# Paired heads in the first mixer, joint chunk operands in the second, and no spin matmuls

## The chip, the cores and the metric

The kernel runs on one core of one Trainium2 chip. The metric is the device time of one execution in microseconds (us), as the median over runs. Engines are written PE (TensorE; PEld is its weight load), DVE (VectorE), ACT (ScalarE), POOL (GpSimd) and SP (SyncE). L553 is line 553 of the kernel's source.

## The reference, cut to what matters

The model is a two-layer backbone over 256 context tokens and 256 latent tokens of width 1024. Layer 0 mixes tokens with a bidirectional Mamba-2 scan and then applies a SwiGLU; layer 1 mixes with bidirectional RWKV-7 and then applies 8 experts of which each token uses 2. For one chunk of 128 tokens and one head the first mixer computes

```python
seg = cum[:, :, :, None] - cum[:, :, None, :]
decay = jnp.exp(jnp.where(lower, seg, -jnp.inf))
cb = jnp.einsum('bcign,bcjgn->bcijg', cm, bm)
w = cb[..., None] * decay * dt[:, :, None]
y = jnp.einsum('bcijge,bcjgep->bcigep', w, x)
```

in each direction, over 32 heads of 64 channels. The second mixer is a recurrence over tokens with a 64x64 state per head (16 heads, two directions, first over the context and then, from the state it left, over the latents):

```python
sa = jnp.einsum('bhvk,bhk->bhv', S, kk_t)
S = S * w_t[:, :, None, :] - sa[..., None] * b_t[:, :, None, :] + v_t[..., None] * k_t[:, :, None, :]
```

## The kernel before, in words

All matmuls are fp32 or a three-product split of fp32 into two fp32r parts. An fp32 matmul stands in the trace as two PE instructions, one for each pass; a PE transpose is one. A tile framework makes the order on each engine: it takes the program's instructions by priority (earlier in the program first) as they become ready in a timeline that it simulates, and it places every semaphore. Tiles of one name in one pool share `bufs` buffers, and the next tile of the name waits until the last reader of the buffer is done.

**First mixer** (L467 to L595). Four groups g, two halves s of each. `project` multiplies a weight slab with the 512 tokens (L212 to L214); `wsplit` makes the two fp32r parts of a slab, the high one on ACT (L206), the low one on the engine it is given (L207): `XE` for the x slabs, `ZE` for the gate slabs. `mix` handles two pairs of heads (m) of its half. For each head e of a pair and each direction d it makes the decays `E` (two bf16 matmuls into `pbc`, then four ACT exponentials, L548), multiplies them with `cb` on DVE into `W` (L550), and adds four matmuls, one for each chunk c, into the PSUM bank `py` (L553). Head e uses the 64 columns of the array that write partitions 64e to 64e+63.

**Second mixer** (L717 to L1567). Heads go in two halves hh of four head pairs; "par" says which head of a pair, and its 64 partitions. Chunks have 64 tokens. The stage generator `stage` runs once for each direction d: `lora` makes rates for two chunks, `decays` makes the running sums `cum` and the decays `Dp`, `operands` makes the tile `BK` (per head two 64-column blocks, from `ta` on DVE at L1060 and from `kd` on POOL at L1061, one instruction for each par) and `KR`, and `grams` multiplies them (L1077 for the latents, L1080 for the context), masks the products into `C` (L1084), and transposes `BK` into `BT` (L1089). `dc` holds each chunk's last decay (L1053). `invert` inverts unit-triangular chunk matrices: a DVE part (L1167, L1170), then three rounds of small 32x32 matmuls (L1197, L1211, L1225). `scan` carries the state through the four chunks. `weave` interleaves generators. The order of the stretches: features and stage of context half 0; its `invert` (called with `warm=(2, 4)`) woven with the stage of context half 1; its scan; features of the latents woven with the inversion and scan of half 1; then for the latents stage 0, inversion 0 woven with the value projection, scan 0 woven with stage 1, inversion 1, scan 1.

With `warm` set, `invert` puts a matmul of the identity (`spin`, L1116: 128x128 weights, 128 columns, fp32) ahead of every second n of the first round and every fourth n of the others, into a part of the PSUM bank that the round itself writes afterwards or doesn't use: 32 in all.

Behind the mixers come the experts (from L1690 on), which stream 1 MB weight tiles through SP's DMA queue; their first loads are issued when the second mixer's pools close.

Of the kernel before, what the change touches and what calls it, by code (L numbers as in the profile page):

```python
# [21 lines left out]
NT = 512  # L22
# [115 lines left out]
def tile_backbone(ctx: ExitStack, tc: tile.TileContext, T, out: bass.AP, dbg=None, stop=99):  # L138
# [227 lines left out]
    with ExitStack() as es:  # L366
# [102 lines left out]
        LATE = ((0, 0), (0, 0), (0, 1), (2, 0))  # L469
        XE, ZE = (V,), (G,)  # L470
        ORDER = ((0, 1, 2, 3), (1, 0, 3, 2))
# [24 lines left out]
        def mix(g, s, px, bf, cf, btm, cb):  # L496
# [38 lines left out]
            for m in range(2):  # L535
                mi = 4 * g + 2 * s + m
                py = bank("py", 1)
                for e in range(2):
                    h = hf + 2 * m + e
                    for d in range(2):  # L540
                        pbc = bank("pbc", 2)
                        PE.matmul(pbc, ehb[:, h:h + 1].to_broadcast([96, 128]), parts[d], start=True, stop=False)
                        PE.matmul(pbc, identb, maskb[:, d:d + 1, :].to_broadcast([128, 4, 128]),
                                  start=False, stop=True)
                        E = mt.tile([128, NT], F32, name="E")
                        for c in range(4):
                            sl = slice(128 * c, 128 * c + 128)
                            S.activation(E[:, sl], pbc[:, sl], AF.Exp, bias=ncum[:, c, 32 * d + h:32 * d + h + 1])  # L548
                        W = mt.tile([128, NT], F32, name="W")
                        V.tensor_mul(W, E, cb)  # L550
                        for c in range(4):
                            sl = slice(128 * c, 128 * c + 128)
                            PE.matmul(py[64 * e:64 * e + 64, sl], xdt[d][:, c, 128 * m + 64 * e:128 * m + 64 * e + 64],  # L553
                                      W[:, sl], start=d == 0 and c == 0, stop=d == 1 and c == 3,
                                      skip_group_check=True)
                V.tensor_add(yz[:, mi, :], yz[:, mi, :], py)
                for d in range(2):
                    h = hf + 2 * m
                    pbc = bank("pbc", 2)
                    PE.matmul(pbc, ehw[:, h:h + 2, :].rearrange("p h q -> p (h q)"), parts[d],  # L560
                              start=True, stop=True)
                    E = mt.tile([128, NT], F32, name="E")
                    S.activation(E, pbc, AF.Exp)
                    p = misc()
                    cs = [c for c in range(4) if c != FIRST[d]]
                    for c in cs:
                        sl = slice(128 * c, 128 * c + 128)
                        PE.matmul(p[:, sl], st[d][c][:, 128 * m:128 * m + 128], cf[:, sl], start=True, stop=True)
                    W = mt.tile([128, NT], F32, name="W")
                    for sl in ((slice(128, 512),) if d == 0 else (slice(0, 128), slice(256, 512))):  # L570
                        V.tensor_mul(W[:, sl], E[:, sl], p[:, sl])
                        V.tensor_add(yz[:, mi, sl], yz[:, mi, sl], W[:, sl])

# [418 lines left out]
    def stage(tp, rp, F, un, d, l2, nb, bks, tags, ready):  # L992
# [4 lines left out]
        o = 1 - d  # L997
        last = 64 if d == 0 else 0
        gr, ms = (lambda: bank(tags[0], 2)), (lambda: bank(tags[1], 2))
# [36 lines left out]
        def decays(c):  # L1036
            th = cur[c // 2][0]
            cum = tp.tile([128, 4, 64], F32, name=f"cum{d}", bufs=nb)
            e = 1 if d == 0 else -1
            V.tensor_tensor_scan(cum.rearrange("p k t -> p (k t)")[:, ::e], smask.rearrange("p k t -> p (k t)"),  # L1040
                                 th[:, c % 2].rearrange("p k t -> p (k t)")[:, ::e], 0.0, op0=ALU.mult, op1=ALU.add)
            Dp = tp.tile([128, 4, 65], F32, name=f"Dp{d}", bufs=nb)
            G.memset(Dp[:, :, 64 * d:64 * d + 1], 1.0)
            S.activation(Dp[:, :, o:o + 64], cum, AF.Exp, scale=-0.3032655)
            S.activation(cum, cum, AF.Exp, scale=0.3032655)
            return Dp, cum

        def operands(c, dd, slot):
            Dp, Di = dd
            _, ta, kd = cur[c // 2]  # L1050
            cs = slice(64 * c, 64 * c + 64)
            cl = slice(64 * (c % 2), 64 * (c % 2) + 64)
            V.tensor_copy(un.dc[d][:, :, c:c + 1], Dp[:, :, last:last + 1])  # L1053
            KR = rp.tile([128, 4, NQ], F32, name=f"KR{slot}")

            BK = bks[d][un.flip[d]]
            un.flip[d] ^= 1
            for par in range(2):
                r, b0 = ROWS[par], 64 * par
                V.scalar_tensor_tensor(BK[par][r, :, b0:b0 + 64], ta[r, :, cl], 0.5, Di[r], op0=ALU.mult, op1=ALU.mult)  # L1060
                G.tensor_mul(BK[par][r, :, 64 - b0:128 - b0], kd[r, :, cl], Di[r])  # L1061
            V.tensor_mul(KR[:, :, 0:64], F["kk"][:, ks, cs], Dp[:, :, d:d + 64])
            if j:
                V.tensor_mul(KR[:, :, 64:128], F["r"][:, ks, cs], Dp[:, :, o:o + 64])
            un.KR[d][c] = KR
            return BK

        def grams(c, BK, slot):
# [5 lines left out]
            for h in range(4):  # L1074
                for par in range(2):
                    if j:
                        PE.matmul(g[par][:, h, :], BK[par][:, h, :], KR[:, h, :], start=True, stop=True)  # L1077
                    else:
                        for z in range(2):
                            PE.matmul(g[par][ROWS[z], h, :], BK[par][:, h, 64 * z:64 * z + 64], KR[:, h, :],  # L1080
                                      start=True, stop=True)
            for par in range(2):
# [4 lines left out]
            for h in range(4):  # L1087
                for par in range(2):
                    PE.transpose(t[par][:, 64 * h:64 * h + 64], BK[par][ROWS[par], h, :],  # L1089
                                 ident[ROWS[par], ROWS[par]])  # L1090
            BT = rp.tile([128, 2, 4, 64], F32, name=f"BT{slot}")
# [21 lines left out]

    def spin(o, x):

        PE.matmul(o[:, :x.shape[1] * x.shape[2]], ident, x, start=True, stop=True)  # L1116

    def invert(tp, un, zbank, slots={}, warm=(0, 0)):


# [68 lines left out]
        for d in range(2):  # L1189
            zb = zbank() if d else z0  # L1190
            z = zb[:, :256].rearrange("p (n t) -> p n t", t=16)
            for n in range(16):
                if warm[0] and n % warm[0] == 0:
                    spin(zb[:, 256:], zp[:, d, n, 0:16].unsqueeze(2).to_broadcast([128, 16, 8]))
                for q in range(4):
                    a, b = (TB[1], zp[:, 1, :, 0:16]) if d else (zp[:, 0], T32[0][:, :, 16:32])
                    PE.matmul(z[QS(q), n, :], a[QS(q), n, :], b[QS(q), n, :], start=True, stop=True)  # L1197
# [5 lines left out]
        for d in range(2):  # L1203
            cb_ = slice(32 * (1 - d), 32 * (1 - d) + 32)
            z = zbank()
            for n in range(16):
                if warm[1] and n % warm[1] == 0 and n < 13:
                    spin(z[:, 32 * n:], TB[d][:, n, :].unsqueeze(2).to_broadcast([128, 32, 4]))
                for par in range(2):
# [7 lines left out]
        for d in range(2):  # L1217
            cb_ = slice(32 * (1 - d), 32 * (1 - d) + 32)
            z = zbank()
            for n in range(16):  # L1220
                if warm[1] and n % warm[1] == 0 and n < 13:
                    spin(z[:, 32 * n:], T32[d][:, n, :].unsqueeze(2).to_broadcast([128, 32, 4]))
                for par in range(2):
                    qa, qb = QA(d, par), QA(1 - d, par)
                    PE.matmul(z[qa, 32 * n:32 * n + 32], zs[qb, d, n, :], T32[d][qb, n, :], start=True, stop=True)  # L1225
# [82 lines left out]
    def operand_tiles(tp):  # L1308
        t = [[tp.tile([128, 2, 4, 128], F32, name=f"BK{d}{i}") for i in range(2)] for d in range(2)]
        for d in t:  # L1310
            for x in d:
                for par in range(2):
                    G.memset(x[:, par], 0.0)
        return [[[x[:, par] for par in range(2)] for x in d] for d in t]

# [16 lines left out]
    with ExitStack() as es:  # L1332
# [28 lines left out]
        with tc.tile_pool(name="r00", bufs=1, side="right", reuse_waits="tile") as r00, tc.tile_pool(name="tp0", bufs=1, reuse_waits="tile") as tp:  # L1361
# [21 lines left out]
            mark("A01T00")  # L1383
            weave((invert(tp, D0, misc, warm=(2, 4)), 1), *stages(tp, r01, F, D1, 1, bks, (("gr", "xu"), ("acc", "xu")), always))
            mark("T01S00")
            slots = {"T": ("BK00", [128, 2, 4, 128]), "M0": ("l2", [128, 2, 512]), "M1": ("BK01", [128, 2, 4, 128])}
            gi = invert(tp, D1, misc, slots)
# [49 lines left out]
    with tc.tile_pool(name="tp2", bufs=1, reuse_waits="tile") as tp:  # L1437
        bks = operand_tiles(tp)
        mark("S10A11")
        L1 = Unit(1, 1, r1, L0.Call)  # L1440
        weave((scan(F, L0, y), 1), *stages(tp, r1, F, L1, 1, bks, SHARED, lambda i: i < L0.steps))
    fks.close()
# [434 lines left out]
```

## Time and profile before

| | us |
|---|---|
| median of 3 runs | 2691.66 |
| runs, lowest and highest | 2684.7 to 2692.46 |
| the profiled execution | 2704.16 |
| its span, first to last instruction | 2702.3 |

| engine | busy us | share of the span | instructions |
|---|---|---|---|
| PE | 2499.3 | 92% | 16810 |
| DVE | 2070.4 | 77% | 3118 |
| ACT | 1455.4 | 54% | 2290 |
| POOL | 416.1 | 15% | 506 |

The shares are averages over stretches with different limits. PE's busy time counts a matmul from its start to the modelled end of its pipeline, so neighbours overlap; how long a matmul holds the engine is seen from the start of the next one. The mean granted TensorE clock of the span is 0.934 of full speed.

### The profile page before, as it was taken

What the parts mean: (1) busy time and instruction counts of PE and PEld (TensorE: products, weight loads), DVE (VectorE), ACT (ScalarE), POOL (GpSimd) and SP (SyncE); (2) the same over time, 40 slices, a digit from 0 to 9 for tenths busy, and PEclk for the clock granted to TensorE, in tenths of its full rate; (3) what the DMA queues carried; (4) which work ended last, traced back from release to release, by engine and by line L of the source; (5) the groups of instructions that cost most, each with busy time, mean ns of one, the idle gap of its engine ahead of it and who ended that gap; (6) DMA issues with size and microseconds to landing.
All of it is one profiled execution on the core that took longest, in us unless ns stands there. A gap on an engine that the chain in (4) does not pass through costs nothing. (4 is left out here: it accounts for less than half of the span.)

```text
span 2702.3 us, 43164 instructions
## 1 busy us (share of the span) xinstructions
PE 2499.3 (92%) x16810; PEld 2043.9 (76%) x16810; DVE 2070.4 (77%) x3118; ACT 1455.4 (54%) x2290; POOL 416.1 (15%) x506
## 2 busy tenths in 40 slices
PE   7999999999999968768977898999999999999997
PEld 4777776778888867558866687788788788878875
DVE  5777788667454377778696745999899899989997
ACT  4444446333222265336343334878787778778775
POOL 1122132110000156224453221000000000000001
PEclk9999999999999978577887877999999999999998
DMA  7322231335554231012110116699899899989983
GB/s 260 114 86 88 78 102 53 132 110 196 177 196 160 65 110 48 1 42 95 41 63 10 57 34 249 262 360 362 326 372 357 330 362 368 358 320 363 372 340 152
DMA packets 99207, 511.54 MB, mean 189 GB/s; under 512 B 11648, under 2 KB 19072, under 8 KB 55216
## 3 DMA queue, kind: packets, MB, share of 16 engines
q1 hardware_dynamic: 97520, 506.52, 51.1%
q8 instruction: 134, 2.20, 0.3%
q10 hardware_dynamic: 1472, 2.16, 0.3%
q14 instruction: 81, 0.66, 0.1%
HBM read 506.54 MB, written 2.10 MB: 188 GB/s over the span
## 5 line engine op out<-in xcount | busy, mean ns | idle before, releaser
L1734 DVE TENSOR_TENSOR wlo<-wraw,whi 128x1024 fp32r<-128x1024 f32 x662 | 798.4, 1224 | 71.3 <-ACT whi L1733 50.6
L1733 ACT CAST whi<-wraw 128x1024 fp32r<-128x1024 f32 x662 | 694.3, 1051 | 209.2 <-PE gu L214 112.0
L213 PE MATMUL gu<-wlo,xg 128*128 128x512 f32 x896 | 355.7, 397 | 1.5 <-DVE wlo L1734 0.7
L214 PE MATMUL gu<-whi,xg 128*128 128x512 f32 x896 | 350.3, 391 | 0.0
L212 PE MATMUL gu<-whi,xg 128*128 128x512 f32 x896 | 336.8, 392 | 1.1 <-ACT xg L1753 0.9
L206 ACT CAST whi<-wraw 128x1024 fp32r<-128x1024 f32 (+2 forms) x126 | 129.5, 1028 | 229.8 <-PE acc L213 216.4
L207 DVE TENSOR_TENSOR wlo<-wraw,whi 128x1024 fp32r<-128x1024 f32 (+2 forms) x110 | 131.7, 1198 | 106.3 <-ACT whi L206 106.2
L213 PEld LDWEIGHTS gu<-wlo,xg 128*128 128x128 f32 x896 | 168.8, 188 | 42.4 <-DVE wlo L1734 5.8
L212 PEld LDWEIGHTS gu<-whi,xg 128*128 128x128 f32 x896 | 168.7, 188 | 38.2 <-ACT xg L1753 1.6
L214 PEld LDWEIGHTS gu<-whi,xg 128*128 128x128 f32 x896 | 168.9, 188 | 31.6
L213 PE MATMUL y<-wlo,HT 128*128 128x512 f32 x448 | 179.1, 400 | 2.3 <-DVE wlo L1734 2.1
L212 PE MATMUL y<-whi,HT 128*128 128x512 f32 x448 | 177.1, 397 | 3.0 <-DVE xg L1754 3.0
L214 PE MATMUL y<-whi,HT 128*128 128x512 f32 x448 | 176.8, 395 | 0.0
L1808 POOL TENSOR_TENSOR wraw<-yx,SH 128x512 f32<-128x512 f32 x4 | 7.5, 1879 | 1025.4 <-DVE yx L1804 1025.4
L212 PE MATMUL acc<-h2hi,whi 128*128 128x512 f32 x352 | 137.3, 393 | 3.4 <-ACT h2hi L343 3.4
L213 PE MATMUL acc<-h2lo,whi 128*128 128x512 f32 x352 | 137.7, 391 | 0.0
L212 PE MATMUL acc<-hhi,whi 128*128 128x512 f32 (+1 forms) x328 | 135.8, 414 | 0.8 <-ACT whi L206 0.8
L214 PE MATMUL acc<-h2hi,wlo 128*128 128x512 f32 x352 | 135.0, 391 | 0.9 <-DVE wlo L207 0.9
L213 PE MATMUL acc<-hlo,whi 128*128 128x512 f32 (+1 forms) x328 | 134.1, 409 | 0.0
L214 PE MATMUL acc<-hhi,wlo 128*128 128x512 f32 (+1 forms) x328 | 133.8, 409 | 0.0
L305 POOL TENSOR_TENSOR sqa<-sqa,sq 128x512 f32<-128x512 f32 (+1 forms) x35 | 46.8, 1338 | 536.0 <-issue 311.9
L777 POOL TENSOR_TENSOR wlo<-wraw,whi 128x512 fp32r<-128x512 f32 (+1 forms) x69 | 86.1, 1257 | 150.3 <-ACT whi L776 138.9
(575 smaller groups left out, 5550.6 us busy)
## 6 DMA issues: line engine op xcount, KB each, us to landing
wraw<-in_w_mi_dram SPq DMA_DIRECT2D x219, 1024.0 KB, 4.9
wraw<-in_w_mo_dram SPq DMA_DIRECT2D x112, 1024.0 KB, 4.9
wraw<-in_w_modT_dram SPq DMA_DIRECT2D x56, 512.0 KB, 4.1
wraw<-in_w_ffi_dram SPq DMA_DIRECT2D x44, 512.0 KB, 3.6
wraw<-in_w_mod_dram SPq DMA_DIRECT2D x40, 512.0 KB, 4.5
wraw<-in_w_mb_dram SPq DMA_DIRECT2D x40, 512.0 KB, 4.3
wraw<-in_w_mbo_dram SPq DMA_DIRECT2D x16, 512.0 KB, 3.5
wraw<-in_w_ffo_dram SPq DMA_DIRECT2D x16, 512.0 KB, 3.5
```

The costliest lines, as they stand in the source:

```text
L206: S.copy(hi, raw)
L207: eng[q % len(eng)].tensor_sub(lo, raw, hi.bitcast(F32))
L212: PE.matmul(o, whi, xhi, start=start, stop=False)
L213: PE.matmul(o, whi, xlo, start=False, stop=False)
L214: PE.matmul(o, wlo, xhi, start=False, stop=stop)
L305: G.tensor_add(self.acc, self.acc, sq)
L777: self.eng[self.n % len(self.eng)].tensor_sub(lo, raw, hi.bitcast(F32))
L1733: S.copy(hi, raw[:, k:k + 2, :])
L1734: V.tensor_sub(lo, raw[:, k:k + 2, :], hi.bitcast(F32))
L1808: G.tensor_mul(xf[:, tt, 512 * n:512 * n + 512], fs, fg[:, 512 * n:512 * n + 512])
```

## The change

In the first mixer the low part of the gate slabs is made by DVE in place of POOL. The loops over direction and head of a pair change places, the two heads' `W` are both made before their matmuls, and the eight matmuls of a pair and direction alternate between the two heads, so between the two column halves; `W` has four buffers in place of two.

In the second mixer `BK` holds for each head two 64-column blocks over all 128 partitions, so that one DVE and one POOL instruction make it, and nothing of it is zero: the memsets go. Each gram matmul of the latents (128 rows, 128 columns) becomes two of 64 rows and 64 columns, each of the context's (128 rows, 64 columns) one of 64 rows and 64 columns, and each transpose becomes two fp32 matmuls with the identity. `dc` comes from an ACT exponential of the running sum in place of a DVE copy out of `Dp`. `cum` and `Dp` have two buffers for each direction in every stage; the last stage has two for `ta` and `kd` as well. The 32 `spin` matmuls are gone.

```diff
-        XE, ZE = (V,), (G,)
+        XE, ZE = (V,), (V,)
...
-                for e in range(2):
-                    h = hf + 2 * m + e
-                    for d in range(2):
+                for d in range(2):
+
+                    Ws = []
+                    for e in range(2):
+                        h = hf + 2 * m + e
                         pbc = bank("pbc", 2)
...
-                        W = mt.tile([128, NT], F32, name="W")
+                        W = mt.tile([128, NT], F32, name="W", bufs=4)
                         V.tensor_mul(W, E, cb)
-                        for c in range(4):
-                            sl = slice(128 * c, 128 * c + 128)
+                        Ws.append(W)
+                    for c in range(4):
+                        sl = slice(128 * c, 128 * c + 128)
+                        for e in range(2):
                             PE.matmul(py[64 * e:64 * e + 64, sl], xdt[d][:, c, 128 * m + 64 * e:128 * m + 64 * e + 64],
-                                      W[:, sl], start=d == 0 and c == 0, stop=d == 1 and c == 3,
+                                      Ws[e][:, sl], start=d == 0 and c == 0, stop=d == 1 and c == 3,
                                       skip_group_check=True)
...
-            cum = tp.tile([128, 4, 64], F32, name=f"cum{d}", bufs=nb)
+            cum = tp.tile([128, 4, 64], F32, name=f"cum{d}", bufs=2)
...
-            Dp = tp.tile([128, 4, 65], F32, name=f"Dp{d}", bufs=nb)
+            Dp = tp.tile([128, 4, 65], F32, name=f"Dp{d}", bufs=2)
             G.memset(Dp[:, :, 64 * d:64 * d + 1], 1.0)
             S.activation(Dp[:, :, o:o + 64], cum, AF.Exp, scale=-0.3032655)
+            end = 63 * o
+            S.activation(un.dc[d][:, :, c:c + 1], cum[:, :, end:end + 1], AF.Exp, scale=-0.3032655)
             S.activation(cum, cum, AF.Exp, scale=0.3032655)
...
-            V.tensor_copy(un.dc[d][:, :, c:c + 1], Dp[:, :, last:last + 1])
...
-            for par in range(2):
-                r, b0 = ROWS[par], 64 * par
-                V.scalar_tensor_tensor(BK[par][r, :, b0:b0 + 64], ta[r, :, cl], 0.5, Di[r], op0=ALU.mult, op1=ALU.mult)
-                G.tensor_mul(BK[par][r, :, 64 - b0:128 - b0], kd[r, :, cl], Di[r])
+            V.scalar_tensor_tensor(BK[:, :, 0], ta[:, :, cl], 0.5, Di, op0=ALU.mult, op1=ALU.mult)
+            G.tensor_mul(BK[:, :, 1], kd[:, :, cl], Di)
...
+        def side(BK, par, h, z):
+
+            return BK[ROWS[par], h, z ^ par, :]
...
-                    if j:
-                        PE.matmul(g[par][:, h, :], BK[par][:, h, :], KR[:, h, :], start=True, stop=True)
-                    else:
-                        for z in range(2):
-                            PE.matmul(g[par][ROWS[z], h, :], BK[par][:, h, 64 * z:64 * z + 64], KR[:, h, :],
-                                      start=True, stop=True)
+                    for z in range(2):
+                        PE.matmul(g[par][ROWS[z], h, :], side(BK, par, h, z), KR[ROWS[par], h, :], start=True, stop=True)
...
-                    PE.transpose(t[par][:, 64 * h:64 * h + 64], BK[par][ROWS[par], h, :],
-                                 ident[ROWS[par], ROWS[par]])
+                    for z in range(2):
+                        PE.matmul(t[par][ROWS[z], 64 * h:64 * h + 64], side(BK, par, h, z),
+                                  ident[ROWS[par], ROWS[par]], start=True, stop=True)
...
-            weave((invert(tp, D0, misc, warm=(2, 4)), 1), *stages(tp, r01, F, D1, 1, bks, (("gr", "xu"), ("acc", "xu")), always))
+            weave((invert(tp, D0, misc), 1), *stages(tp, r01, F, D1, 1, bks, (("gr", "xu"), ("acc", "xu")), always))
...
-        weave((scan(F, L0, y), 1), *stages(tp, r1, F, L1, 1, bks, SHARED, lambda i: i < L0.steps))
+        weave((scan(F, L0, y), 1), *stages(tp, r1, F, L1, 2, bks, SHARED, lambda i: i < L0.steps))
```

## Rows read from the trace of the kernel before

**Rows 1.** Busy time by stretch: PE, PEld, DVE, ACT, POOL, granted clock, DMA share, GB/s.
```profile
100.00:476.00 376.00, 368.24 (x2048) 276.49 (x2046) 294.36 (x511) 180.24 (x428) 92.74 (x75) 1.00 0.23 79
...
1020.00:1085.00 65.00, 53.07 (x574) 46.74 (x573) 50.51 (x103) 36.66 (x100) 36.12 (x53) 0.92 0.12 42
1085.00:1115.40 30.40, 15.97 (x181) 13.62 (x181) 30.10 (x85) 12.00 (x36) 9.21 (x15) 0.67 0.00 1
...
1115.40:1153.20 37.80, 37.80 (x578) 28.99 (x578) 15.44 (x29) 7.59 (x16) 7.67 (x12) 0.50 0.01 2
...
1158.50:1172.20 13.70, 8.41 (x184) 6.84 (x184) 10.90 (x44) 5.44 (x15) 2.92 (x15) 1.00 0.25 74
...
1348.00:1393.00 45.00, 31.79 (x240) 27.10 (x238) 38.49 (x69) 19.37 (x57) 30.39 (x43) 0.90 0.10 36
1446.00:1530.00 84.00, 73.30 (x1068) 63.90 (x1062) 57.52 (x111) 38.37 (x107) 28.47 (x46) 0.88 0.01 2
...
1700.00:2600.00 900.00, 891.88 (x4042) 733.34 (x4043) 834.20 (x808) 702.60 (x755) 0.00 (x0) 0.99 0.92 350
```

**Rows 2.** Timeline of PE, first mixer: start us, us until the last end, what, [idle before].
```profile
209.76 1.96 PE L553 MATMUL py<-W,xdt 128*64 128x128 f32 x16
...
239.75 1.09 PE L553 MATMUL py<-W,xdt 128*64 128x128 f32 x8
```

**Rows 3.** Timeline of PE at 1159 us, gram matmuls of the context.
```profile
1158.86 1.15 PE L1080 MATMUL gr<-KR,BK 128*64 128x64 f32 x32
1159.84 0.40 PE L1080 MATMUL acc<-KR,BK 128*64 128x64 f32 x6
```

**Rows 4.** Instruction groups, 96 to 478 us: count | busy us, mean ns | idle before.
```profile
L548 ACT ACTIVATE E<-pbc,ncum 128x128 f32<-128x128 f32 x256 | 73.0, 375 | 50.0 <-DVE W L571 34.5 <-PE pbc L543 10.1 <-DVE mods L250 2.6
...
L207 POOL TENSOR_TENSOR wlo<-wraw,whi 128x1024 fp32r<-128x1024 f32 x14 | 36.8, 2632 | 62.1 <-ACT whi L206 62.1
...
L207 DVE TENSOR_TENSOR wlo<-wraw,whi 128x1024 fp32r<-128x1024 f32 x21 | 26.4, 1256 | 8.2 <-ACT whi L206 8.2
```

**Rows 5.** Instruction groups of DVE, 1020 to 1085 us.
```profile
L1060 DVE SCALAR_TENSOR_TENSOR BK<-ta,cum 64x256 f32<-64x256 f32 x16 | 10.6, 664 | 0.9 <-ACT cum L1045 0.6
...
L1053 DVE COPY dc<-Dp 128x4 f32<-128x4 f32 x8 | 3.7, 468 | 0.0
```

**Rows 6.** Instruction groups of POOL, 1003 to 1030 us.
```profile
L1313 POOL MEMSET BK<- 128x512 f32 x8 | 3.8, 524 | 8.5 <-PE gr L801 7.9 <-DVE mx L860 0.5
```

**Rows 7.** Instruction groups of DVE, 1085 to 1115.4 us.
```profile
L1060 DVE SCALAR_TENSOR_TENSOR BK<-ta,cum 64x256 f32<-64x256 f32 x8 | 4.8, 600 | 0.1
```

**Rows 8.** Timeline of PE at 1117 us, inside the inversion with spins.
```profile
1117.53 0.80 PE L1116 MATMUL ms<-T,cst 128*128 128x128 f32 x2
1118.26 0.41 PE L1197 MATMUL ms<-M,T 32*32 32x16 f32 x16
```

**Rows 9.** Instruction groups, 1115 to 1155 us.
```profile
L1116 PE MATMUL ms<-T,cst 128*128 128x128 f32 x32 | 12.7, 501 | 5.5 <-DVE T L1185 5.5
```

**Rows 10.** Waits, 1110 to 1170 us: us in total, times, longest.
```profile
POOL BK L1061 <- PE xu L1089: 20.1, 2, 19.5
```

**Rows 11.** Timeline of PE, the latents' first inversion (no spins): first and last round.
```profile
1427.98 1.26 PE L1197 MATMUL xu<-T,M 32*32 32x16 f32 x88 [4.15 <-DVE T L1185]
...
1445.37 1.19 PE L1225 MATMUL ms<-M,T 32*32 32x32 f32 x62
```

**Rows 12.** Instruction groups of DVE, 1348 to 1393 us.
```profile
L1060 DVE SCALAR_TENSOR_TENSOR BK<-ta,cum 64x256 f32<-64x256 f32 x14 | 8.7, 620 | 0.2
...
L1053 DVE COPY dc<-Dp 128x4 f32<-128x4 f32 x7 | 4.4, 628 | 0.7 <-ACT Dp L1044 0.7
```

**Rows 13.** Timeline at 1039 us: the eight transposes of a context chunk.
```profile
1039.59 0.46 PE L1089 MATMUL ms<-cst,BK 64*128 64x64 f32 x8
```

**Rows 14.** Instruction groups of ACT, whole span: an instruction on few columns.
```profile
L1498 ACT ACTIVATE rv<-ms,epsg 128x8 f32<-128x8 f32 x4 | 1.1, 268 | 2.5 <-PE ms L1495 2.4
```

**Rows 15.** Waits, 1446 to 1530 us.
```profile
POOL Dp L1043 <- DVE KR L1064: 6.8, 4, 2.7
```

More of the change, by code (lines that the diff above doesn't have):

```diff
@@ L568, in mix @@
                         PE.matmul(p[:, sl], st[d][c][:, 128 * m:128 * m + 128], cf[:, sl], start=True, stop=True)
-                    W = mt.tile([128, NT], F32, name="W")
+                    W = mt.tile([128, NT], F32, name="W", bufs=4)
                     for sl in ((slice(128, 512),) if d == 0 else (slice(0, 128), slice(256, 512))):
@@ L997, in stage @@
         o = 1 - d
-        last = 64 if d == 0 else 0
         gr, ms = (lambda: bank(tags[0], 2)), (lambda: bank(tags[1], 2))
@@ L1112, in stage, with invert @@
             yield from grams(c, BK, 2 * i + d)
-    def spin(o, x):
-        PE.matmul(o[:, :x.shape[1] * x.shape[2]], ident, x, start=True, stop=True)
-    def invert(tp, un, zbank, slots={}, warm=(0, 0)):
+    def invert(tp, un, zbank, slots={}):
         def tile_(name, n):
@@ L1192, in invert @@
             for n in range(16):
-                if warm[0] and n % warm[0] == 0:
-                    spin(zb[:, 256:], zp[:, d, n, 0:16].unsqueeze(2).to_broadcast([128, 16, 8]))
                 for q in range(4):
@@ L1206, in invert @@
             for n in range(16):
-                if warm[1] and n % warm[1] == 0 and n < 13:
-                    spin(z[:, 32 * n:], TB[d][:, n, :].unsqueeze(2).to_broadcast([128, 32, 4]))
                 for par in range(2):
@@ L1220, in invert @@
             for n in range(16):
-                if warm[1] and n % warm[1] == 0 and n < 13:
-                    spin(z[:, 32 * n:], T32[d][:, n, :].unsqueeze(2).to_broadcast([128, 32, 4]))
                 for par in range(2):
@@ L1308, in operand_tiles @@
     def operand_tiles(tp):
[L1309 to L1314, printed above, removed]
+        return [[tp.tile([128, 4, 2, 64], F32, name=f"BK{d}{i}") for i in range(2)] for d in range(2)]
     def stages(tp, rp, F, un, nb, bks, tags, ready, l2=None):
@@ L1383, in tile_backbone @@
             mark("A01T00")
-            weave((invert(tp, D0, misc, warm=(2, 4)), 1), *stages(tp, r01, F, D1, 1, bks, (("gr", "xu"), ("acc", "xu")), always))
+            weave((invert(tp, D0, misc), 1), *stages(tp, r01, F, D1, 1, bks, (("gr", "xu"), ("acc", "xu")), always))
             mark("T01S00")
-            slots = {"T": ("BK00", [128, 2, 4, 128]), "M0": ("l2", [128, 2, 512]), "M1": ("BK01", [128, 2, 4, 128])}
+            slots = {"T": ("BK00", [128, 1024]), "M0": ("l2", [128, 2, 512]), "M1": ("BK01", [128, 1024])}
             gi = invert(tp, D1, misc, slots)
```

## The prediction

> **What bounds the kernel now.** I first read the busy time by stretch, since the page's shares average over stretches with different limits. In the first mixer PE is busy 368 of 376 us at full clock and DVE 294, so PE is the bound and DVE has 82 us free [rows 1]. In the second mixer the bound changes. In the first stage (1020 to 1085 us) DVE works 50.5 of 65 us and PE 53.1. In the DVE part of the first inversion DVE works 30.1 of 30.4 us. In its matmul part PE is busy 37.8 of 37.8 us at half clock, while DVE works 15.4 and ACT 7.6. In the latents' first stage DVE works 38.5 of 45 us, and in their second one, beside a scan, PE 73.3 of 84 [rows 1]. The experts then run in a steady state, with PE at 892 of 900 us and DMA at 0.92 [rows 1]; nothing in them changes and their loads start when the second mixer ends, so I let every microsecond saved ahead of them pass through to the end.
>
> Next I read PE's timeline where the change touches it, for the start-to-start time and not the duration. Last come the groups of DVE and POOL by stretch, and the waits.
>
> **First mixer, pairing.** A run of 16 of the old `py` instructions takes 1.96 us until its last end, 0.12 us each [rows 2]. They all use the same column half, and one pass of 128 fp32 columns follows another. The context's grams alternate between the halves, with 64 columns: 32 of them start within 0.98 us, 31 ns each, at full clock [rows 1, 3]. Twice that, for 128 columns, is 61 ns against 122. So a second half does run beside the first, and a fully paired run of 16 takes about 0.98 us in place of 1.96. The 512 instructions hold PE for 32 such runs, so full pairing gives 31 us.
>
> I don't expect all of it. The planner takes the first ready instruction by priority. The trace holds the 512 in 55 runs, of which 10 have 16 instructions and 39 have 8, like the ones in [rows 2]. A run of 8 is one `W`, sent as soon as it was planned ready, with other work behind it before the next `W`. In the new program the first head's four matmuls are then still ready first and go out unpaired. Only where both `W` were ready, the 10 runs of 16, do I count the pairing: 10 x 0.98 = 9.8, taken as **-9.4**. The bounds are 0 and -31.
>
> **First mixer, the gate slabs.** Sixteen low parts (14 of them in the window) go from POOL at 2.63 us to DVE at 1.26 us [rows 4]. That is 20 us more for DVE, which has 82 free, and POOL, which is in nobody's way, gives up 42. I take **+1**, bounds 0 and +30 (the rival on DVE's queue, below). Four `W` buffers only free DVE from waiting for PE: nothing, with a bound of a few us.
>
> **Context, stage 0.** `BK` takes DVE 16 instructions, 10.6 us, and `dc` 8, 3.7 us [rows 5]. Half of the first and all of the second go: 9.0 us. DVE is busy 78% and PE 82% of this stretch, so half passes: **-4.5**. POOL's eight memsets take 3.8 us just ahead of its first rate instructions [rows 6]; half: **-2**. POOL's own `BK` instructions halve too; POOL is free enough there that I count nothing, bound -4.
>
> **Context, stage 1 beside the inversion's DVE part.** DVE is the bound outright [rows 1]. Half of 4.8 us of `BK` [rows 7] and four `dc` at 0.47 us [rows 5] are 4.3 us; I take **-3.5**, bounds 0 and -4.3.
>
> **The spins.** From the start of a spin (two instructions) to that of the next small matmuls pass 0.73 us [rows 8]; there are 32 (the row of 32 instructions [rows 9] and as many again in the later rounds). 32 x 0.73 = 23.4 of the 37.8 us. The stretch is PE's: POOL waits 19.5 us in one piece to refill a `BK` buffer whose transposes stand behind the inversion in PE's queue [rows 10]. What is late next is the chain between the rounds, of PE, DVE and ACT. The latents' first inversion runs the same rounds without spins, also in part at half clock, from 1427.98 to 1446.56 us, 18.6 us with other work in between [rows 11]. 37.8 - 18.6 = 19.2, so I take **-19.2**, bounds -10 (the work of the stage that now falls between the rounds) and -23.4.
>
> A row that bears on this: the clock was granted at half for the whole 37.8 us in which the spins kept PE busy [rows 1]. [...] The sum above goes by the row.
>
> **Latents, stage 0.** `BK` 8.7 us and `dc` 4.4 us on DVE [rows 12]: 4.35 + 4.4 = 8.75 us of a stretch that DVE fills to 86%. At 0.6: **-5.2**, bounds -2 and -9.
>
> **Latents, stage 1.** The same relief of about 9 us, but PE has the stretch, so a quarter: **-2**. The transposes get dearer. Eight took 0.46 us [rows 13]; now they are 16 fp32 matmuls, 32 instructions, which at 31 ns [rows 3] take 0.99: half a microsecond for each of 32 chunks and directions. Where DVE is the bound PE's gaps hide it; here, eight times 0.5: **+4**. If the gaps didn't hide it, +16 in all.
>
> The grams themselves I price at nothing. An fp32 matmul's two passes use one tile of the array and follow each other, and the rows of the context show one matmul for each pass time already with two halves (31 ns x 2 for 64 columns [rows 3]). With passes in order, four tiles give no more than two.
>
> **`dc` on ACT and the double buffers.** An ACT instruction on few columns takes 0.27 us [rows 14], 8.6 us over 32; it stands between the two exponentials, so a chunk's `BK` comes 0.27 us later. Against it the next chunk's sums no longer wait for the last one's readers; in the latents' second stage such waits were 6.8 us [rows 15]. I take 0 for both, bounds -7 and +9.
>
> **Sum.** -9.4 + 1 - 4.5 - 2 - 3.5 - 19.2 - 5.2 - 2 + 4 = -40.8 us. From the profiled execution, 2704.16, this gives 2663.4. That execution was 12.5 us above the median of the runs shown, 2691.66, so for a median I say **2651**, its own range 2632 to 2670. A measurement of this kernel can tell about 0.3%, 8 us, from no change.
>
> **The rivals.**
> *Full pairing.* Speaks for it: `W` of both heads are often done well before PE gets to them. Against: 39 runs of 8. It adds 31 - 9.4 = 21.6 us: 2629. Chance 0.20.
> *Four tiles at once.* The passes of different tiles could overlap more than I read, as the grams now use all four quarters. For it speaks nothing in the rows, which show one pass time per matmul. The transposes' +4 would vanish and the context grams' 0.98 us for a chunk [rows 3] halve, of which some 8 of 16 lie on the path: -8, 2643. Chance 0.05. [...]
> *The clock falls behind the inversion.* After the spins the clock was full from 1158.5 to 1172.2 us, with 8.4 us of PE work [rows 1]. If the sparser matmuls no longer bring it up, that work doubles, and perhaps as much again later in the scan: +17, 2668. Against it: the clock rose only when the grams came, not in the spins. Chance 0.11.
> *DVE's queue stands.* POOL waited 62 us for ACT's high parts before its 14 low parts [rows 4]. On DVE such a wait stops everything behind it (the convolutions, `W`, the states). If two thirds of it gets through to PE, the 40 are gone: about 2691. Against: DVE's own 21 low parts waited only 8.2 us [rows 4]. Chance 0.11.
> *PE waits for the second head.* This one ends slower. If the planner does put the pairs alternately but ACT is late, PE's queue stands at the second head's first matmul, and the projections behind it too. The place is L553, the price one wait in each of 32 pairs. A head's exponentials take 4 x 0.375 = 1.5 us on ACT [rows 4], at ACT's other load easily 3: 96 us, less 31 from the pairing and 32.4 from the second mixer, gives +33, 2725. It decides from about 2 us per pair. Against it: PE has a backlog of projections and the old `py` runs hardly waited. Chance 0.10.
>
> **How the numbers follow.** My own case has 0.43; faster cases are it, full pairing, four tiles and the clock: 0.79. No change is the standing queue, 0.11; slower is the waiting PE, 0.10. The range 2620 to 2690 takes in all of the faster cases and leaves out the last and the worse half of the queue's, some 0.17.
>
> **What would show it.** Right: the first context inversion's matmuls take 15 to 20 us in place of 38 and POOL's long wait is gone; `BK` counts halve on DVE and POOL at about the same duration each; gram instructions cost PE what they did and the transposes twice; in the first mixer a minority of `py` runs alternate at 61 ns. Wrong: most `py` runs alternating (then 20 us more), PE idle ahead of `py`, DVE idle ahead of the low parts, or half clock long after the inversion.

## The result, and the profile after

The changed kernel takes 2652.66 us in the median (2645.93 to 2658.37), the kernel before 2689.55 beside it: ratio 0.9864, 95% interval 0.9831 to 0.9897. The forecast was 2651 in 2620 to 2690. The total fits by luck: two of its largest terms do not fit, and their errors cancel.

The profiled execution took 2658.37 us, its span is 2656.5. Against the 2702.3 of before, in us, by the starts of the first instruction of each part in the two timelines (the spans differ by 45.8 and the medians by 36.9, so some 9 us of the differences are the two executions' own):

| part | before | after | difference |
|---|---|---|---|
| ahead of the first `pbc` matmul | 94.7 | 96.7 | +2.0 |
| first mixer, to its first output part (L610) | 383.8 | 361.5 | -22.3 |
| projection, first feed-forward, features, to the first running sum | 544.9 | 540.1 | -4.8 |
| context stage 0, to the last mask | 52.9 | 48.3 | -4.6 |
| inversion's DVE part, to its first small matmul | 39.9 | 33.4 | -6.5 |
| small matmuls, to the first scan matmul | 46.7 | 40.6 | -6.1 |
| scan, second inversion, features of the latents | 166.6 | 166.1 | -0.5 |
| latents stage 0, to the last mask | 59.4 | 58.3 | -1.1 |
| inversion 0 and value projection, to the first mask of stage 1 | 84.3 | 83.7 | -0.6 |
| latents stage 1, first to last mask | 53.4 | 49.6 | -3.8 |
| inversion 1, last scan | 105.5 | 113.0 | +7.5 |
| experts to the end | 1070.2 | 1065.2 | -5.0 |

Busy time by stretch of the changed kernel, columns as in [rows 1]:

```profile
100.00:456.00 356.00, 346.81 (x2066) 254.96 (x2064) 292.10 (x528) 180.68 (x432) 59.42 (x62) 1.00 0.26 83
...
998.00:1046.00 48.00, 42.96 (x678) 40.02 (x682) 33.50 (x63) 26.33 (x75) 28.83 (x42) 0.89 0.16 56
...
1046.60:1080.00 33.40, 11.84 (x188) 9.77 (x182) 31.97 (x95) 14.51 (x47) 6.49 (x11) 0.65 0.00 1
...
1080.00:1110.30 30.30, 24.18 (x636) 21.56 (x636) 14.97 (x26) 16.76 (x45) 6.19 (x8) 0.50 0.01 3
...
1296.00:1345.00 49.00, 35.97 (x671) 29.67 (x668) 36.09 (x63) 17.01 (x59) 27.15 (x38) 0.79 0.01 2
...
1538.00:1591.00 53.00, 52.02 (x879) 46.05 (x881) 24.19 (x61) 16.27 (x42) 12.60 (x16) 0.91 0.13 42
...
1700.00:2600.00 900.00, 891.66 (x4043) 732.28 (x4042) 834.91 (x807) 703.61 (x755) 0.00 (x0) 0.99 0.94 354
```

PE still fills the first mixer. The DVE part of the inversion is still DVE's (31.97 of 33.40). In the matmul part the spins that filled PE are gone: PE 24.18 of 30.30, DVE 14.97, ACT 16.76, so no engine is the bound there. PE's timeline shows what stands in it, and the pairs:

```profile
136.08 0.43 PE L557 MATMUL py<-W,xdt 128*64 128x128 f32 x2
...
139.67 1.09 PE L557 MATMUL py<-W,xdt 128*64 128x128 f32 x14
...
149.80 1.09 PE L557 MATMUL py<-W,xdt 128*64 128x128 f32 x16
...
1081.33 0.71 PE L1192 MATMUL ms<-M,T 32*32 32x16 f32 x36
1081.98 0.80 PE L1013 MATMUL xu<-hw,l 128*128 128x128 f32 x2
1082.57 0.63 PE L1014 MATMUL xu<-ha,l 128*128 128x128 f32 x2
1083.13 0.29 PE L1192 MATMUL ms<-M,T 32*32 32x16 f32 x4
...
1104.45 1.91 PE L1204 MATMUL ms<-M,C 32*32 32x32 f32 x64 [5.54 <-DVE M L1195]
...
1121.90 0.97 PE L1091 MATMUL xu<-cst,BK 64*64 64x64 f32 x32
...
1303.98 1.10 PE L1082 MATMUL gr<-KR,BK 64*64 64x128 f32 x32
...
1472.31 0.69 PE L1091 MATMUL ms<-cst,BK 64*64 64x64 f32 x32
```

A run of 16 `py` instructions is over in 1.09 us, against 1.96 [rows 2]. Most pairs go out as 2 and 14: one matmul of the first head, other work, then the rest alternating. The small matmuls are broken up by `lora` pairs of the next stage, and PE then stands 5.54 us for DVE's transpose. A chunk's grams of the latents, 32 quarter instructions, are over in 1.10 us. In before the same products took 1.95 (PE's timeline there, granted clock 1.00 in both):

```profile
1348.52 1.95 PE L1077 MATMUL gr<-KR,BK 128*128 128x128 f32 x16
```

So the quarters do the same products in little more than half the time of full tiles. The 32 instructions of a chunk's transposes take 0.69 or 0.97 us until the last end, against 0.46 for the eight of before [rows 13].

Groups, columns as in [rows 4]: the low slab parts (96 to 458 us), `BK` and `dc` (998 to 1046), `lora` in the matmul part (1080 to 1110.3):

```profile
L207 DVE TENSOR_TENSOR wlo<-wraw,whi 128x1024 fp32r<-128x1024 f32 x34 | 42.7, 1257 | 9.5 <-ACT whi L206 9.4
...
L1061 DVE SCALAR_TENSOR_TENSOR BK<-ta,cum 128x256 f32<-128x256 f32 x8 | 4.7, 613 | 0.0
...
L1049 ACT ACTIVATE dc<-cum 128x4 f32<-128x4 f32 x8 | 1.5, 194 | 0.0
...
L1013 PE MATMUL xu<-hw,l 128*128 128x128 f32 x16 | 6.4, 502 | 0.0
L1014 PE MATMUL xu<-ha,l 128*128 128x128 f32 x16 | 5.1, 421 | 0.0
```

DVE makes 34 low parts and waits 9.5 us for ACT, so the standing queue did not come. `BK` has half the instructions of [rows 5] at about the same length, and `dc` costs ACT 194 ns. POOL's wait of [rows 10] is down from 19.5 us to 8.3:

```profile
POOL BK L1062 <- PE xu L1091: 8.3, 1, 8.3
```

### The profile page after: what moved, and what is told of

Same layout as the page of the kernel before. It is cut to its first block, busy times and chain, and to the rows that moved or that the text cites. A ratio compares the mean times of both kernels' runs of the same rounds, so it can differ in the third digit from the quotient of the medians.

```text
span 2656.5 us, 44879 instructions
## 1 busy us (share of the span) xinstructions
PE 2440.9 (92%) x17770; PEld 1994.8 (75%) x17770; DVE 2039.1 (77%) x3070; ACT 1457.5 (55%) x2322; POOL 341.9 (13%) x434
## 3 DMA queue, kind: packets, MB, share of 16 engines
q1 hardware_dynamic: 97520, 506.52, 52.8%
## 5 line engine op out<-in xcount | busy, mean ns | idle before, releaser
L206 ACT CAST whi<-wraw 128x1024 fp32r<-128x1024 f32 (+2 forms) x126 | 129.7, 1030 | 218.4 <-PE acc L213 206.2
L207 DVE TENSOR_TENSOR wlo<-wraw,whi 128x1024 fp32r<-128x1024 f32 (+2 forms) x126 | 151.8, 1205 | 110.0 <-ACT whi L206 109.8
L260 DVE SCALAR_TENSOR_TENSOR wraw<-wraw,scb 128x1024 f32<-128x1024 f32 x56 | 68.5, 1223 | 50.2 <-DMA wraw<-in_w_modT_dram 49.4
```

The costliest lines, as they stand in the source:

```text
L206: S.copy(hi, raw)
L207: eng[q % len(eng)].tensor_sub(lo, raw, hi.bitcast(F32))
L260: V.scalar_tensor_tensor(t, w, 0.5, scb[:, j, :], op0=ALU.mult, op1=ALU.mult, accum_out=mods[l][:, n, j:j + 1])
```

## The experiments

M stands for the first mixer's edits, S for the removal of the spins, O for the second mixer's operands (joint `BK`, quarter grams, `dc` on ACT, second buffers). The stretches are those of the table above, from one profile each; ratios are to the kernel before on the same chip, where its median was 2691.54 to 2693.75 in the experiments, so rows are compared by ratio first.

| kernel | median us | ratio, 95% | first mixer | stage 0 | DVE part | small matmuls to scan |
|---|---|---|---|---|---|---|
| before | 2689.55 | | 383.8 | 52.9 | 39.9 | 46.7 |
| changed (M, S, O) | 2652.66 | 0.9864 (0.9831 to 0.9897) | 361.5 | 48.3 | 33.4 | 40.6 |
| M | 2667.42 | 0.9899 (0.9880 to 0.9917) | 360.4 | 54.4 | 39.9 | 46.1 |
| S | 2678.74 | 0.9949 (0.9931 to 0.9967) | 383.8 | 51.9 | 39.7 | 28.3 |
| O | 2690.98 | 0.9992 (0.9979 to 1.0005) | 383.9 | 49.4 | 33.2 | 60.6 |
| M, O | 2661.23 | 0.9910 (0.9884 to 0.9935) | 360.8 | 49.4 | 34.1 | 60.5 |
| M, S | 2663.96 | 0.9899 (0.9878 to 0.9919) | 361.0 | 55.0 | 39.2 | 28.9 |
| pairing without slabs | 2692.78 | 0.9997 (0.9981 to 1.0013) | 367.5 | 61.5 | 40.1 | 45.8 |
| slabs without pairing | 2695.17 | 1.0005 (0.9990 to 1.0019) | 381.4 | 52.8 | 39.8 | 46.7 |
| M, not alternating | 2685.31 | 0.9971 (0.9957 to 0.9985) | 369.3 | 50.3 | 40.1 | 47.0 |
| changed, inversion first | 2651.66 | 0.9851 (0.9837 to 0.9866) | 360.4 | 49.2 | 33.5 | 41.9 |
| changed, one-pass transposes | 2655.61 | 0.9861 (0.9843 to 0.9878) | 360.2 | 50.1 | 33.7 | 33.7 |
| changed, single buffers | 2650.35 | 0.9849 (0.9827 to 0.9871) | 361.2 | 48.0 | 33.7 | 38.5 |
| changed, both of these orders | 2650.62 | 0.9832 (0.9817 to 0.9848) | 360.8 | 50.2 | 33.8 | 32.0 |

**M alone.** The diff's edits from L467 to L575; the rest as before.

> The kernel before with the first mixer's edits alone (paired heads, the low gate slabs on DVE, four W buffers); the second mixer as before. The prediction's step (only the runs of 16 pair, a gain of 8.4 us) gives about 2681 beside a median of 2689.6. Theory A, from the profile after (the first mixer ends 22.3 us earlier, nearly all runs alternate): about 2667, the instructions of the pairs hold PE for about 42 us in place of 64, and everything behind the first mixer keeps its length.

2667.42, a gain of about 1%: theory A. The first mixer is 23.4 us shorter.

**Pairing without the slabs.**

```diff
-        XE, ZE = (V,), (V,)
+        XE, ZE = (V,), (G,)
```

> The kernel before with the first mixer's pairing and four W buffers, but the gate slabs' low parts left on POOL; the second mixer as before. If the pairing makes the whole gain of the first mixer and the slabs cost or bring nothing (the prediction's +1): 2666 to 2667. If DVE's 20 us more had cost something: faster than that, 2660. If PE's shorter runs then wait for POOL's low parts: 2675 to 2680, and PE is idle ahead of the projections.

None of these: no gain at all. The first mixer is 16.3 us shorter (383.8 to 367.5), 7.1 less than with the slabs on DVE. Then context stage 0, which no edit touched, is 8.6 us longer. Its order on DVE had changed, since the framework orders by its own timeline, which the edit shifts; in 1008 to 1070 us DVE now waited for ACT ahead of a low part of the value projection, a wait that the same stage of before does not show:

```profile
DVE BT L781 <- ACT BT L780: 9.2, 2, 6.7
DVE cum L1044 <- POOL th L1024: 3.1, 1, 3.1
```

The remaining 8 us stand in this profile (span 2693.5 against 2702.3), but the profiled execution of before was 12.5 us above the median of its own runs; that this order cost the gain is argued from one profile, not shown.

**Slabs without pairing.**

```diff
-        XE, ZE = (V,), (G,)
+        XE, ZE = (V,), (V,)
```

> The kernel before with nothing changed but that the gate slabs' low parts are made by DVE. The prediction's step gives +1 us: 2692. Theory B, from the runs with pairing alone (no gain) and with all of the first mixer's edits (25 us): the slabs on POOL held back PE, and their move alone wins 5 to 10 us in the first mixer: about 2684. Rival C: the slabs count only once the pairing has made PE shorter: 2692, with the first mixer as long as before.

2695.17, no change, and the first mixer 2.4 us shorter: close to rival C. The slabs are worth 2 us as long as the pairs are long and 7 once they are short (367.5 against 360.4).

**M, not alternating.**

```diff
-                    for c in range(4):
-                        sl = slice(128 * c, 128 * c + 128)
-                        for e in range(2):
+                    for e in range(2):
+                        for c in range(4):
+                            sl = slice(128 * c, 128 * c + 128)
```

> The first mixer as in the changed kernel (both W made first, four buffers, slabs on DVE), except that the eight matmuls of a pair and direction go out head by head, four and four, not alternating; the second mixer as before. If the alternation of the column halves makes the gain: about 2690, and the pairs hold PE for about 64 us again. If a part came from the buffers, the slabs or the loop order: 2667 to 2680.

Between the two: the alternation holds 8.9 us of the first mixer's length (369.3 against 360.4) and some 70% of its gain in the total. The rest is not the loop order's alone. On this kernel's PE timeline a full run of 16, first head and then second, takes

```profile
183.51 1.58 PE L557 MATMUL py<-W,xdt 128*64 128x128 f32 x16
```

1.58 us, where 16 of the same column half take 1.96 [rows 2] and 16 alternating 1.09: in this order some passes of the second head already run beside the first's.

**S alone.**

```diff
-            weave((invert(tp, D0, misc, warm=(2, 4)), 1), *stages(
+            weave((invert(tp, D0, misc), 1), *stages(
```

> The kernel before with the spins of the first context inversion taken out, nothing else. The prediction's step gives -19.2 us: 2670. Rival B: what falls between the rounds now (the next stage's matmuls) and the DVE chain of that stage keep most of it, and the gain is 7 us or less: 2683. Rival C: the clock pays for it later, half speed lasts longer behind the inversion, and nothing is gained: 2690.

A gain of 0.51%, 13.7 us: between the step and rival B. Where the spins stood the step is right: 46.7 to 28.3 us to the first scan matmul, 18.4 less. The stretch of the small matmuls by the busy time:

```profile
1113.80:1134.10 20.30, 13.48 (x540) 12.54 (x540) 18.06 (x31) 8.33 (x18) 9.58 (x14) 0.50 0.01 3
```

**O alone, and M with O.** The changed kernel with the spins put back, in the first case with the first mixer of before.

> The kernel before with the second mixer's operands alone: joint BK, grams and transposes in quarters, dc on ACT, two buffers for sums and decays; the spins stay, the first mixer is as before. The prediction's steps for these are -4.5 -2 -3.5 -5.2 -2 +4 = -13.2 us: 2676. Rival B: the relief of DVE is worth nothing where PE or the chain between chunks binds, and only the memsets' 4 us and the latents' second stage are won: about 2683. Rival C: the dearer transposes take back all of it: 2690, and the last inversion with its scan is longer by some 8 us as in the changed kernel.

> The changed kernel with the spins of the first context inversion put back, nothing else. If taking them out is worth 19 us in the new kernel: 2672 beside 2652.7. If the stage beside it binds anyway: 2660 or less. If the clock after it gives the gain back: 2653.

O alone gains nothing (rival C in the total), though stage 0 is 3.5 us shorter and the DVE part 6.7. Ahead of stage 0 another 5.6 are won (544.9 to 539.3). Of these 15.8 us 13.9 come back in the small matmuls, 46.7 to 60.6. Their stretch in the kernel with O alone:

```profile
1100.20:1150.30 50.10, 50.10 (x687) 39.40 (x686) 14.49 (x26) 16.64 (x45) 6.22 (x8) 0.50 0.01 2
```

PE is busy for all of 50.10 us at half clock. In before the stage's second `lora` ran in the DVE part (1076.3 to 1116.1), in PE's gaps, and none of it in the matmul part. The group rows of before, in the DVE part:

```profile
L1010 PE MATMUL xu<-hw,l 128*128 128x128 f32 x28 | 7.2, 341 | 2.4 <-ACT ta L1014 2.4
L1011 PE MATMUL xu<-ha,l 128*128 128x128 f32 x28 | 5.8, 292 | 0.0
```

With O the DVE part is shorter, and half of these instructions (16 and 16, 11.5 us of PE in the changed kernel's rows above) land between the rounds. With M and O the median is 2661.23, so the spins cost the new kernel 8.6 us by medians, nearest to the second guess, and 12 by the ratios (0.9910, 0.9864), whose intervals overlap; their stretch differs by 19.9 (60.5 against 40.6).

**M and S, operands as before.**

> The kernel before with the first mixer's edits and without the spins, the second mixer's operands as before: the changed kernel without joint BK, quarter grams, dc on ACT and second buffers. The prediction's terms for those, -13 us, give 2666 here. Theory B, that they are worth nothing because the chain between chunks and the inversion's rounds set the end and not DVE: 2653, and the scan of the first context half starts within 3 us of the changed kernel's 1120.6.

2663.96: near the prediction's 2666 and not theory B. O is worth 11.3 us by medians beside M and S. The intervals overlap (0.9878 to 0.9919, 0.9831 to 0.9897), but the changed kernel with single buffers, which was measured beside this one, lies clear of it (2650.35; 0.9827 to 0.9871). So the joint operands win some 13 us once M and S are in. O wins nothing alone and, by ratio, nothing beside M with the spins (0.9910 against 0.9899; by medians 6.2). Theory B falls in its place too: the scan starts at 1124.4, 3.8 us behind the changed kernel. The small matmuls here, and the stretch of the second inversion and the latents' features, with the same stretch of M alone below:

```profile
1095.50:1118.10 22.60, 15.21 (x568) 14.02 (x570) 19.74 (x34) 9.87 (x21) 11.75 (x17) 0.50 0.02 4
...
1195.00:1293.60 98.60, 96.76 (x1140) 84.22 (x1139) 66.90 (x129) 46.95 (x113) 39.31 (x50) 0.74 0.22 74
```

```profile
1208.80:1299.70 90.90, 85.12 (x1139) 75.18 (x1138) 65.64 (x131) 47.93 (x113) 38.78 (x49) 0.85 0.23 78
```

The same 1139 or 1140 matmuls take 98.60 us at a granted clock of 0.74 and 90.90 at 0.85. So of the 17.2 us that S brings to M at the scan (46.1 to 28.9), 7.7 are gone in a stretch that no edit touched; by medians 3.5 are left, by ratio nothing (0.9899 twice). That taking the spins out lowers this clock is not shown: with S alone the same stretch kept 0.85:

```profile
1214.00:1305.10 91.10, 86.81 (x1139) 75.20 (x1138) 65.19 (x129) 47.94 (x113) 37.89 (x49) 0.85 0.23 77
```

**Inversion first.** The woven inversion gets priority over the stage.

```diff
-            weave((invert(tp, D0, misc), 1), *stages(
+            weave((invert(tp, D0, misc), 1, 1000), *stages(
```

> The changed kernel with the first context inversion put ahead of the stage woven with it, by priority; the same work. Theory A, that the stage's matmuls and DVE work between the rounds hold back the rounds and with them all that follows: the matmul part takes about 20 us in place of 30, the scan starts up to 10 us earlier, about 2643. Rival B: the stage's work is only pushed behind the rounds and its end sets the start of what follows: 2652, no change, with a short matmul part and the same end of the stage.

Rival B: 2651.66. The rounds are compact, and the stage's rest stands behind them:

```profile
1076.60:1094.40 17.80, 15.42 (x585) 14.48 (x585) 5.22 (x9) 6.87 (x15) 2.42 (x4) 0.50 0.02 5
1094.40:1118.50 24.10, 15.12 (x326) 13.39 (x324) 14.49 (x29) 15.56 (x46) 8.49 (x18) 0.65 0.01 2
```

17.80 and 24.10 us instead of 30.3 and 10.3: the scan starts no sooner after the first small matmul (41.9 against 40.6).

**One-pass transposes.** `BK` transposed with `PE.transpose`, eight for a chunk and direction; two copies put the second head's halves in place.

```diff
-                    for z in range(2):
-                        PE.matmul(t[par][ROWS[z], 64 * h:64 * h + 64], side(BK, par, h, z),
-                                  ident[ROWS[par], ROWS[par]], start=True, stop=True)
+                    PE.transpose(t[par][:, 64 * h:64 * h + 64], BK[ROWS[par], h].rearrange("p z t -> p (z t)"),
+                                 ident[ROWS[par], ROWS[par]])
...
-            for par in range(2):
-                S.copy(BT[:, par], t[par][:, :256].rearrange("p (h q) -> p h q", h=4))
+            S.copy(BT[:, 0], t[0][:, :256].rearrange("p (h q) -> p h q", h=4))
+            for z in range(2):
+                S.copy(BT[ROWS[z], 1], t[1][ROWS[1 - z], :256].rearrange("p (h q) -> p h q", h=4))
```

> The changed kernel with BK transposed as before, by eight one-pass transposes for a chunk and direction in place of 16 two-pass matmuls; the second head's two halves then change places in the copy to BT, one more ACT instruction for each. If the dearer transposes cost the prediction's 4 us: 2648. If the whole 0.5 us for each of 32 lies on the path: 2637. If PE's gaps hide them everywhere: 2653, or up to 8 us more, since ACT has 32 copies more.

2655.61, the third case. The small matmuls are 6.9 us shorter, since more of PE's work lies in the DVE part (first row: PE 16.96 us, 11.84 in the changed kernel), but the latents' first stage loses 5.2 (39.8 to 45.0 us from first to last mask):

```profile
1045.10:1078.80 33.70, 16.96 (x189) 13.80 (x190) 32.62 (x97) 19.84 (x61) 7.22 (x11) 0.64 0.01 1
...
1295.50:1340.50 45.00, 33.54 (x328) 25.66 (x328) 30.62 (x49) 14.35 (x47) 21.72 (x32) 0.56 0.00 1
```

PE has two thirds of the instructions there and runs at 0.56 of full clock (second row), against 498 instructions and 0.74 in the changed kernel's 1305 to 1345 us.

**Single buffers.** `cum`, `Dp` and the last stage's rates with one buffer, `dc` copied on DVE.

```diff
-            cum = tp.tile([128, 4, 64], F32, name=f"cum{d}", bufs=2)
+            cum = tp.tile([128, 4, 64], F32, name=f"cum{d}", bufs=nb)
...
-            S.activation(un.dc[d][:, :, c:c + 1], cum[:, :, end:end + 1], AF.Exp, scale=-0.3032655)
+            V.tensor_copy(un.dc[d][:, :, c:c + 1], Dp[:, :, last:last + 1])
```

> The changed kernel with one buffer for each direction's sums and decays and for the rates of the last stage, and dc copied by DVE, as before; the joint operands, the pairing and the missing spins stay. The prediction prices the second buffers and dc on ACT together at 0, between -7 and +9, with the relief of DVE's 0.47 us copies counted in the stages: 2655 to 2665. If DVE's relief is worth nothing here either: 2653. If the second buffers are the useful part: 2660 or more.

2650.35, the second case: second buffers and `dc` on ACT bring nothing.

**Both orders.** Priority and one-pass transposes together.

> The changed kernel with both the one-pass transposes and the first context inversion put ahead by priority. In single profiles the stretch from the inversion's first small matmul to the first scan matmul took 28 to 29 us without spins and with the old operands, 40.6 in the changed kernel, 41.9 with the priority, 33.7 with one-pass transposes. Theory A, that the dearer transposes and the stage's work between the rounds together give back what the operands win ahead of it: 30 us or less, and about 2645. Rival B: the stage's own chain ends the stretch at 33 us or more whatever the order, and with the clock's lot behind it the time is 2652, as the other three variants of the changed kernel.

2650.62 (2640.19 to 2655.78), rival B. The stretch falls to 32.0 us; the latents' first stage then takes 43.6 at a clock of 0.66:

```profile
1298.70:1342.30 43.60, 30.56 (x327) 23.54 (x328) 30.57 (x48) 14.30 (x47) 21.90 (x32) 0.66 0.00 1
```

Its interval touches that of the changed kernel, so none of the four variants is shown to be faster.

## Why the prediction came out right, point by point

- **Pairing, -9.4 predicted; 16 us of the first mixer alone and 21 beside the slabs (381.4 to 360.4).** The pace was nearly right (a run of 16 in 1.09 us; 0.98 predicted). The count was not: the prediction took the ten runs of 16 for places where both heads' `W` were ready, but none of them took less than 1.96 us, where a run that changes heads takes 1.58, so they were runs of one head, in its two directions. The step that failed is "the first head's four matmuls are then still ready first and go out unpaired". The program's order in the changed kernel has one matmul of the first head (`W_852`), ten instructions of other work, then seven that alternate:

```
372 L557 MATMUL py_843<-W_852,xdt0_677 64x128
373 L572 MATMUL misc_916<-cf_556,st12_758 128x128
...
383 L557 MATMUL py_843<-W_862,xdt0_677 64x128
384 L557 MATMUL py_843<-W_852,xdt0_677 64x128
385 L557 MATMUL py_843<-W_862,xdt0_677 64x128
```

  The second matmul of the first head was ready and did not go: matmuls into one `py` bank stay in the order of the program. This is the rival "full pairing" (2629), and its sign, most `py` runs alternating. It came to 22 of its 31 us: by the starts in the two traces the 512 instructions hold PE for 42.4 us in place of 64.6, and a first or last matmul still goes alone in 20 runs of two.
- **Gate slabs, +1 predicted; -2 alone and -7 beside the pairing.** Inside the first mixer this move is a gain. What holds PE back without it is not shown: PE's waits in the run with pairing alone name no low part of POOL, and the longest is 3.6 us, for DVE's `st`.
- **Stage 0 of the context, -6.5 predicted; -4.6 in it and -4.8 ahead of it.** The 3.8 us of memsets [rows 6] pass in full: with O alone the time from the first `lora` matmul to the first running sum is 12.0 us against 17.0.
- **DVE part, -3.5 predicted, -6.5 measured,** more than the 4.3 us of DVE work removed: half of the `lora` work left this stretch as well, and DVE is busy 31.97 us there in place of 38.39 (1076.3 to 1116.1 in before).
- **The spins, -19.2 predicted; -6.1 in the stretch of the small matmuls.** The size of the spins was right: taking them out shortens the stretch by 18.4 us alone, 17.2 beside M and 19.9 beside M and O. What failed is that the terms were added as if apart: O lengthens the same stretch by 13.9 (14.4 beside M), because `lora` moves into the rounds. The bound of -10 for "the work of the stage that now falls between the rounds" named this and was too small. With the rounds put first the stage's rest stands behind them and the stretch is no shorter. In the total S brings 13.7 us alone, by ratio nothing beside M and 12 beside M and O; how much of the difference is the clock behind it stays open.
- **Latents, stage 0: -5.2 predicted, -1.1 measured.** DVE was relieved (38.49 of 45 us [rows 1], 36.09 of 49 after), and little came of it. Over the kernels it took 56.7 to 58.5 us with O, 62.0 and 63.4 with the one-pass transposes, and 57.7 to 62.8 without O. What ends it now was not settled; its clock was 0.79, and one wait of PE for POOL's `rk` grew from 4.0 to 6.0 us. **Stage 1: +2 predicted, -3.8 measured,** which shows nothing: from first to last mask it took 46.4 to 56.0 us in the kernels with O and 48.8 to 55.7 in those without. Of the +7.5 behind it 3.8 are no term of the change: the last scan took 53 us at a clock of 0.91 here, but 49.2 at full clock in before and in seven of the other kernels, the one with O alone and that with M and O among them.
- **Grams 0, transposes +4.** "With passes in order, four tiles give no more than two" failed: the latents' grams take 1.10 us in place of 1.95 where all four quarters alternate at full clock, 0.85 less for each of at most 16 chunks and directions, and a chunk's 32 transpose instructions take 0.69 us where they are fastest, with 0.99 predicted and 0.46 for the eight of before [rows 13]. The rival "four tiles at once" is what PE did: the same products 1.77 times as fast (1.95 / 1.10). How much of it reached the end is not shown: the latents' second stage, which was PE's, took about as long with O as without. The one-pass transposes won nothing (2655.61).
- **`dc` and second buffers, 0:** within the measurement (2650.35).
- **The rivals.** DVE's queue did not stand and PE did not wait for second heads (no wait of PE at L557 for `W` longer than 0.9 us). The clock behind the inversion was lower in places, as feared, but single stretches were longer with it by 4 to 8 us and no more (49.2 to 53 us at 1.00 and 0.91, 90.90 to 98.60 at 0.85 and 0.74). (The part that the range leaves out, 0.10 and half of 0.11, is 0.155 and not "some 0.17".)

The sum was close by luck: 14 us too little in the first mixer stood against some 13 too much in the small matmuls, and the other terms, -13.2 us in the prediction, are -14.4 in this one pair of profiles (-4.8 - 4.6 - 6.5 - 0.5 - 1.1 - 0.6 - 3.8 + 7.5, to the end of the last scan).

## What to carry over

When matmuls of two heads add into one PSUM bank, in this framework the order written in the program decides the pairing, not which operand is ready first. Before counting a relief of the engine that bounds a stretch, ask which other engine used that stretch as its cover: here PE did its `lora` matmuls behind DVE, and they reappeared between the rounds of the inversion. Time the parts alone and together: here pairing alone and slabs alone gave nothing, and both together 1%; beside them the missing spins and the joint operands gave nothing one at a time, and together 0.35 to 0.5%.

## What the hardware showed that was not expected

- Sixteen instructions of one column half take 1.96 us, eight of one half followed by eight of the other 1.58, alternating 1.09.
- By the profile's count PE was busy for 50.10 of 50.10 us at half the clock (0.50, O alone), with 687 instructions, 32x32 and 128x128 fp32 matmuls mixed, and for 346.81 of 356.00 us at 1.00 in the first mixer of the changed kernel. So here a busy PE came with either clock.
- The same stretch of 1139 matmuls was granted 0.74 to 0.85 of full clock in kernels that do not differ in it, 98.60 against 90.90 us. That is more than most of the edits here were worth, so a gain of a few us is to be read from the stretch and from medians, not from one span.
